# Hybrid encoder on one core: softmax normalised once per pair of heads, by rows that TensorE makes, instead of once per block of probabilities

## The chip, the cores and the metric

The kernel runs on one core of a Trainium2 chip. A core has TensorE (matrix products and transposes), VectorE, ScalarE, GpSimd and SyncE, which issues transfers; each runs its own queue of instructions in order. The metric is the device time in microseconds (us) of one execution. In the profile's rows PE is TensorE's matmul, PEld its weight load, DVE VectorE, ACT ScalarE, POOL GpSimd and SP SyncE; "SPq" is SyncE's DMA queue.

## The reference

Two layers over a sequence of 512 with width 1024; a conditioning vector gives shift, scale and gate for both halves of a layer. Attention has 8 dilated heads and 8 latent heads (MLA); then comes an MLP of width 4096. Shortened:

```python
for l in range(2):
    h = rms_norm(x, g_norm_mix) * (1 + sc1) + sh1
    q_d, k_d, v_d, cq, ckv, k_rope = split(h @ w_in)
    o_dil = dilated_attention(rms_norm(q_d), rms_norm(k_d), v_d, positions, slopes)  # 8 heads of 64
    o_mla = latent_attention(cq, ckv, k_rope, positions, ...)                        # 8 heads, rotary part of 32
    x = x + gt1 * (concat[o_dil, o_mla] @ w_out)
    h = rms_norm(x, g_norm_mlp) * (1 + sc2) + sh2
    x = x + gt2 * (relu(h @ w_mlp_in) ** 2 @ w_mlp_out)
# each head: p = exp(s - max s);  l = sum(p);  o = (p @ v) / l
```

A dilated head's score has a bias of slope times distance of the positions, and the mixture over three dilations comes down to one softmax with a further table of logarithms in the bias. The latent heads rotate 32 of their 96 score columns by angles of the positions.

## The kernel before, in words

**Layout.** Activations are transposed: x is 8 tiles of [128, 512], width on the partitions. For accuracy every operand of a product is split into a high and a low part: `load_split` loads a weight tile `raw` and makes `wh` (ScalarE, L233) and `wl` (GpSimd, L234). `mm3` issues three matmuls for each product (L238 to L240). All weights are streamed by SyncE.

**Attention.** Each layer has 8 stages `st`, one for each pair of heads: 0 to 3 dilated, 4 to 7 latent. `heads` runs `head` for both heads of the pair. A head has 4 steps, one for each block of 128 queries, 128 steps in the whole kernel. A step runs: score matmuls into `sc`; the maximum on VectorE (L346, or with the bias added in the same instruction, L343); the exponential on ScalarE, which also gives the sum l_ (L347, L344); the reciprocal r_ on VectorE (L348); P times r_, by a table `NRM` on ScalarE (L351, 56 steps), VectorE (L353, 8) or GpSimd (L355, 64); four transposes of P on TensorE (L358); a high copy on ScalarE (L361) and the low rest on VectorE (L362). Behind the four steps stand the products with the values (L368), and ScalarE and VectorE put the head's 64 rows into `o` (L370, L371). At the pair's end `o` is split into `ot`, high on ScalarE (L628) and low on GpSimd (L629). The output projection reads `ot`.

**What lies between the steps.** `weave` puts pieces of the next pair's projection, weight loads, the output projection's first half and layer 1's modulation between the steps, at places that the table `TUNE` gives. From this program a planner of the framework sets the final order on every engine, and the semaphores; a change of the code can therefore move instructions that it does not touch.

**Buffers.** Tiles of one tag share a ring of buffers (`BUFS`, L61): `s` has two, `P` three, `o` one. In PSUM, tag `mm` has four banks, `sc` (scores) two, `tr` (transposes of P, products with the values) two. A tile that takes a buffer waits for the last reader of the tile that had it.

**The start of layer 0's attention.** The latent part is transposed and split into `ct` tiles (`ot` tag, L527, L528). `rope_tables` makes the rotary tables of queries and keys from a gain `g` (loaded at L482) by five small GpSimd operations each (L487 to L491) into tiles `rot` of their own; L535 to L538 rotate the keys `kr` (written at L512). `distances` loads the row of positions `posr` into an `s` tile (L307); VectorE cuts it into 16-bit halves (L312, L313) and converts them (L314), and from these come the distances for the biases.

Of the kernel before, what the change touches and what calls it, by code (L numbers as in the profile page):

```python
# [9 lines left out]
F32 = mybir.dt.float32  # L10
F32R = mybir.dt.float32r
I32 = mybir.dt.int32
AF = mybir.ActivationFunctionType
# [15 lines left out]

NRM = (('AAGG', 'GAGA'), ('GAGA', 'GAVG'))

TUNE = dict(
    F0=(0, 0), F1=(6.4, 2.33), T0=(3.23, 2.08), T1=(8.8, 8.8), M0=(0, 0), M1=(4, 4), M2=(4.1, 4.1),
    M3=(6.5, 6.55), LD0=(5, 5), LD1=(9, 9), LM=(6.45, 7.11), LO=(7.2, 7.2), OD0=(3.1, 3.1), OD1=(5.1, 5.1),
# [6 lines left out]
def trunk(ctx: ExitStack, tc: tile.TileContext, a):  # L43
# [12 lines left out]
    def nm(p):  # L56
# [1 line left out]
        return f"{p}{uid[0]}"  # L58


    BUFS = dict(h=8, qk=8, ot=8, pt=4, zz=2, raw=3, wh=4, wl=4, P=3, b=2, s=2, o=1, st=9, hs=9,  # L61
                mm=4, sc=2, tr=2)

    def t4(tag, shape, dt=F32R):
# [259 lines left out]
        SY.dma_start(g, a["lnc"])  # L324
        return dist, g

    def head(l, h, hd, score, bias, vals, o):
        pt = [(t4("pt", [128, 4, 256]), t4("pt", [128, 4, 256])) for _ in range(2)]
        for qb in range(4):
            sc = ps("sc")  # L330
            score(hd, sc, qb)
            m, l_, r_ = (small(1, "hs") for _ in range(3))
            P = s2(tag="P")
            if bias:
                b = s2(tag="b")
                if l == 0:
                    dist, g = bias
                    A.activation(b, dist[qb // 2][:, qb % 2], AF.Abs, scale=SLOPES[h])
                    G.tensor_tensor(b, b, g[:, 384 - 128 * qb:896 - 128 * qb], op=OP.add)
                    SY.dma_start(bias_d[h][qb], b)  # L340
                else:
                    SY.dma_start(b, bias_d[h][qb])
                V.tensor_tensor_reduce(P, sc, b, op0=OP.add, op1=OP.min, scale=1.0, scalar=3e38, accum_out=m)  # L343
                A.activation(P, P, AF.Exp, bias=m, scale=-1.0, accum_out=l_)  # L344
            else:
                V.tensor_reduce(m, sc, axis=AX.X, op=OP.max, negate=True)  # L346
                A.activation(P, sc, AF.Exp, bias=m, scale=1.0, accum_out=l_)  # L347
            V.reciprocal(r_, l_)  # L348
            e_ = NRM[l][bool(bias)][qb]
            if e_ == "A":  # L350
                A.activation(P, P, AF.Copy, scale=r_)  # L351
            elif e_ == "V":
                V.tensor_scalar(P, P, r_, None, op0=OP.mult)  # L353
            else:
                G.tensor_scalar(P, P, r_, 0.0, op0=OP.mult, op1=OP.add)  # L355
            tr = ps("tr", (128, 4, 128))
            for kc in range(4):
                T.transpose(tr[:, kc], P[:, kc * 128:(kc + 1) * 128], ident)  # L358
            c0 = (qb % 2) * 128
            hi, lo = (t[:, :, c0:c0 + 128] for t in pt[qb // 2])  # L360
            A.activation(hi, tr, AF.Copy)  # L361
            V.tensor_tensor(lo, tr, f(hi), op=OP.subtract)  # L362
            yield
# [14 lines left out]
    for l in range(L):  # L378
# [99 lines left out]


        def rope_tables(src, is_k):  # L480
            g = col(NR, "gr")
            SY.dma_start(g, bass.AP(tensor=src.tensor, offset=src.offset, ap=[[0, 128], [1, NR]]))  # L482
            C = rot(2 * is_k)
            Sn = rot(2 * is_k + 1)
            ga = g[:, 0:16].rearrange("p (o d) -> p o d", o=1).to_broadcast([128, 4, 16])
            gb = g[:, 16:32].rearrange("p (o d) -> p o d", o=1).to_broadcast([128, 4, 16])
            G.tensor_tensor(C[:, :, 0], cos, ga, op=OP.mult)  # L487
# [134 lines left out]
        def heads(st, w):  # L622
            pr, bias = st % 4, (bias0 if l == 0 else True) if st < 4 else None
            o = s2(tag="o")
            for hd in range(2):
                yield from head(l, 2 * pr + hd, hd, w["score"], bias, w["vals"], o)
            ot = t4("h" if st in (2, 3) else "ot", [128, 2, S])
            A.activation(ot[:, 0], o, AF.Copy)  # L628
            G.tensor_tensor(ot[:, 1], o, f(ot[:, 0]), op=OP.subtract)  # L629
            OT.append(ot)  # L630
# [302 lines left out]
```

## Time and profile before

| | before |
|---|---|
| device time, median of 3 runs (all) | 1374.31 us (1374.08 to 1374.61) |
| profiled execution, its own time | 1371.87 us |
| span of its instructions | 1370.1 us |
| TensorE matmul busy | 1274.0 us, 93% |
| TensorE weight loads busy | 1106.1 us, 81% (beside the matmuls) |
| VectorE / ScalarE / GpSimd busy | 762.4 / 683.7 / 662.0 us (56 / 50 / 48%) |
| mean granted clock of TensorE | 0.974 |

Rows of the profile that group instructions give the line, engine, operation, what it writes and reads with shapes, the count, then busy time and the mean of one in ns, then the engine's idle time just before them and what ended it ("<-POOL P L355" is the write of P by GpSimd at line 355). Rows of single instructions begin with start and length in us, and end in brackets with the idle time before them. "x4" is a run of four. Rows of a stretch A:B give its length, then the busy time of PE, PEld, DVE, ACT and POOL, the granted clock (1.00 is full), the DMA engines' busy share and GB/s.

### The profile page before, as it was taken

How to read it: one execution, taken by the hardware profiler on the slowest of the kernel's cores; microseconds unless marked ns; L12 is line 12 of the kernel's file. 1: busy time of each engine (PE TensorE's matmuls, PEld its weight loads, DVE VectorE, ACT ScalarE, POOL GpSimd, SP SyncE). 2: the span in 40 equal slices, each digit the busy share in tenths (PEclk: the TensorE clock that was granted, in tenths of full speed). 3: DMA queues.
4: the chain of work that ended last, by engine and by line, in shares of the span. 5: the costliest groups of instructions: out<-in, count | busy, mean ns of one | idle time of the engine just before them, and what ended most of it. 6: DMA issues, size and time to landing. Idle time of an engine off the chain costs nothing.

```text
span 1370.1 us, 19443 instructions
## 1 busy us (share of the span) xinstructions
PE 1274.0 (93%) x6922; PEld 1106.1 (81%) x6922; DVE 762.4 (56%) x1732; ACT 683.7 (50%) x1453; POOL 662.0 (48%) x600
## 2 busy tenths in 40 slices
PE   3889878888999999999998999899889999999999
PEld 2877867777988888888888999788788888888888
DVE  6687887786653481743576577998562122121223
ACT  5578787876442231322235577888654233232321
POOL 5646686663454444444436244455246444444441
PEclk7989998999999999999999999999999999999999
DMA  9325553232235483754533244311013223222321
GB/s 344 112 88 184 165 160 101 87 108 73 98 123 185 149 280 108 235 203 133 181 124 89 89 122 145 93 47 47 17 62 106 94 93 101 99 92 97 104 92 62
DMA packets 57248, 167.61 MB, mean 122 GB/s; under 512 B 8640, under 2 KB 10816, under 8 KB 57152
## 3 DMA queue, kind: packets, MB, share of 16 engines
q1 hardware_dynamic: 57152, 166.38, 37.3%
q8 instruction: 54, 0.88, 0.3%
q14 instruction: 42, 0.34, 0.1%
HBM read 155.87 MB, written 10.49 MB: 121 GB/s over the span
## 4 chain that ended last, share of the span: by engine, by line
PE 73%; DVE 6%; ACT 6%; issue 4%; POOL 3%; DMA 3%; POOLq 0%; DVEq 0%; ACTq 0%
PE mm L238 21%; PE mm L239 21%; PE mm L240 21%; PE tr L368 2%; PE tr L358 2%; POOL wl L234 2%; DMA raw<-in_wout_dram 1%; DVE pt L362 1%; DVE raw L170 1%; DMA raw<-in_wup_dram 1%; ACT pt L361 1%; PE sc L238 1%; ACT P L347 1%; PE mm L603 1%; PE sc L239 1%
## 5 line engine op out<-in xcount | busy, mean ns | idle before, releaser
L234 POOL TENSOR_TENSOR wl<-raw,wh 128x1024 fp32r<-128x1024 f32 (+3 forms) x188 | 425.7, 2268 | 454.9 <-ACT wh L233 433.1
L233 ACT ACTIVATE wh<-raw 128x1024 fp32r<-128x1024 f32 (+3 forms) x188 | 188.7, 1004 | 272.6 <-PE mm L240 202.7
L636 DVE SCALAR_TENSOR_TENSOR x<-mm,mod,x 128x512 f32<-128x512 f32 (+1 forms) x144 | 89.3, 630 | 261.7 <-PE mm L240 261.2
L238 PE MATMUL mm<-h,wh 128*128 128x512 f32 (+1 forms) x608 | 224.5, 370 | 7.1 <-ACT h L274 7.1
L239 PE MATMUL mm<-h,wl 128*128 128x512 f32 (+1 forms) x608 | 224.4, 370 | 0.0
L240 PE MATMUL mm<-h,wh 128*128 128x512 f32 (+1 forms) x608 | 222.1, 369 | 1.6 <-POOL h L271 1.1
L238 PE MATMUL mm<-ot,wh 128*128 128x512 f32 (+1 forms) x448 | 155.2, 348 | 4.3 <-ACT ot L628 4.1
L239 PE MATMUL mm<-ot,wl 128*128 128x512 f32 (+1 forms) x448 | 154.0, 345 | 0.0
L240 PE MATMUL mm<-ot,wh 128*128 128x512 f32 (+1 forms) x448 | 152.6, 347 | 0.2 <-POOL ot L629 0.2
L809 ACT ACTIVATE P<-mm 128x512 f32<-128x512 f32 (+1 forms) x72 | 39.2, 551 | 203.2 <-PE mm L240 203.2
L238 PEld LDWEIGHTS mm<-h,wh 128*128 128x128 f32 x608 | 116.1, 191 | 25.9 <-ACT h L274 7.5
L240 PEld LDWEIGHTS mm<-h,wh 128*128 128x128 f32 x608 | 114.6, 190 | 21.1 <-POOL h L271 1.5
L239 PEld LDWEIGHTS mm<-h,wl 128*128 128x128 f32 x608 | 116.1, 191 | 19.1 <-POOL wl L234 0.3
L810 DVE SCALAR_TENSOR_TENSOR mm<-mm,P 128x512 f32<-128x512 f32 (+1 forms) x72 | 45.4, 635 | 139.5 <-ACT P L809 139.5
L238 PE MATMUL mm<-wh,h 128*128 128x384 f32 (+1 forms) x288 | 97.0, 352 | 16.5 <-ACT h L719 9.8
L238 PE MATMUL mm<-qk,wh 128*128 128x512 f32 (+1 forms) x288 | 105.2, 366 | 1.0 <-DVE x L636 1.0
L239 PE MATMUL mm<-qk,wl 128*128 128x512 f32 (+1 forms) x288 | 105.2, 365 | 0.0
L240 PE MATMUL mm<-qk,wh 128*128 128x512 f32 (+1 forms) x288 | 105.2, 365 | 0.0
L239 PE MATMUL mm<-wh,h 128*128 128x384 f32 (+1 forms) x288 | 99.8, 349 | 5.3 <-POOL h L722 3.2
L240 PE MATMUL mm<-wl,h 128*128 128x384 f32 (+1 forms) x288 | 99.3, 347 | 0.8 <-POOL wl L234 0.8
L170 DVE SCALAR_TENSOR_TENSOR pt<-pt,cb 128x1024 f32<-128x1024 f32 x56 | 99.2, 1806 | 0.0
L238 PEld LDWEIGHTS mm<-ot,wh 128*128 128x128 f32 x448 | 85.3, 190 | 15.2 <-ACT ot L628 4.5
(248 smaller groups left out, 2673.3 us busy)
## 6 DMA issues: line engine op xcount, KB each, us to landing
raw<-in_w_dram SPq DMA_DIRECT2D x64, 512.0 KB, 3.4
pt<-in_wmod_dram SPq DMA_DIRECT2D x56, 512.0 KB, 4.9
raw<-in_w2a_dram SPq DMA_DIRECT2D x48, 512.0 KB, 3.5
raw<-in_wmod_dram SPq DMA_DIRECT2D x24, 512.0 KB, 3.7
raw<-in_win_dram SPq DMA_DIRECT2D x30, 384.0 KB, 3.1
bias<-b SPq DMA_DIRECT2D x32, 256.0 KB, 2.3
raw<-in_wout_dram SPq DMA_DIRECT2D x16, 512.0 KB, 3.7
raw<-in_w2b_dram SPq DMA_DIRECT2D x16, 512.0 KB, 3.3
```

Of the source, the lines that this page charges most:

```text
L170: r = V.scalar_tensor_tensor(w, w, 1.0, cb, op0=OP.mult, op1=OP.mult, accum_out=out)
L233: A.activation(hi, raw, AF.Copy)
L234: G.tensor_tensor(lo, raw, f(hi), op=OP.subtract)
L238: T.matmul(out, sh, mh, start=first, stop=False)
L239: T.matmul(out, sl, mh, start=False, stop=False)
L240: T.matmul(out, sh, ml, start=False, stop=last)
L347: A.activation(P, sc, AF.Exp, bias=m, scale=1.0, accum_out=l_)
L358: T.transpose(tr[:, kc], P[:, kc * 128:(kc + 1) * 128], ident)
L368: T.matmul(po[:, HALF[qh]], vals(hd, kc), pt[qh][w][:, kc], start=(kc == 0 and w == 0), stop=(kc == 3 and w == 1))
L636: V.scalar_tensor_tensor(xT[j][:, hf], p, gt[:, j:j + 1], xT[j][:, hf], op0=OP.mult, op1=OP.add)
L809: A.activation(r, p, AF.Relu)
L810: V.scalar_tensor_tensor(p, p, 0.0, r, op0=OP.max, op1=OP.mult)
```

## The change

The scaling of P goes out. The sums of a pair's 8 steps go into one tile `den` [128, 8], queries on the partitions. At the pair's end VectorE inverts it into `rc`; ScalarE spreads the values into `wide` [128, 4, 2, 64] (an `s` tile); TensorE transposes the four blocks into a bank of tag `mm`, where the inverted sums now lie as rows along the queries, 64 equal rows for each head; VectorE multiplies `o` by them. Only then is `o` split. `o` gets a second buffer. Besides, the keys' rotary tables move from tiles of their own into an `s` tile, and the gain `g` of all four tables shares one buffer.

```diff
-NRM = (('AAGG', 'GAGA'), ('GAGA', 'GAVG'))
...
-    BUFS = dict(h=8, qk=8, ot=8, pt=4, zz=2, raw=3, wh=4, wl=4, P=3, b=2, s=2, o=1, st=9, hs=9,
+    BUFS = dict(h=8, qk=8, ot=8, pt=4, zz=2, raw=3, wh=4, wl=4, P=3, b=2, s=2, o=2, st=9, hs=6, den=4,
...
-    def head(l, h, hd, score, bias, vals, o):
+    def head(l, h, hd, score, bias, vals, o, den):
...
-            m, l_, r_ = (small(1, "hs") for _ in range(3))
+            m, l_ = small(1, "hs"), den[:, 4 * hd + qb:4 * hd + qb + 1]
...
-            V.reciprocal(r_, l_)
-            e_ = NRM[l][bool(bias)][qb]
-            if e_ == "A":
-                A.activation(P, P, AF.Copy, scale=r_)
-            elif e_ == "V":
-                V.tensor_scalar(P, P, r_, None, op0=OP.mult)
-            else:
-                G.tensor_scalar(P, P, r_, 0.0, op0=OP.mult, op1=OP.add)
...
         def rope_tables(src, is_k):
-            g = col(NR, "gr")
+            g = const.tile([128, NR], F32, tag="gr", name=nm("gr"))
             SY.dma_start(g, ...)
-            C = rot(2 * is_k)
-            Sn = rot(2 * is_k + 1)
+            if is_k:
+                both = s2([128, 2, 4, 2, 16])
+                C, Sn = both[:, 0], both[:, 1]
+            else:
+                C, Sn = rot(0), rot(1)
...
             o = s2(tag="o")
+            den, rc = small(8, "den"), small(8, "den")
             for hd in range(2):
-                yield from head(l, 2 * pr + hd, hd, w["score"], bias, w["vals"], o)
+                yield from head(l, 2 * pr + hd, hd, w["score"], bias, w["vals"], o, den)
+
+            V.reciprocal(rc, den)
+            wide = s2([128, 4, 2, 64])
+            A.activation(wide, rc.rearrange("p (h q o) -> p q h o", h=2, o=1).to_broadcast([128, 4, 2, 64]), AF.Copy)
+            rows = ps("mm", (128, 4, 128))
+            for qb in range(4):
+                T.transpose(rows[:, qb], wide[:, qb].rearrange("p h d -> p (h d)"), ident)
+            V.tensor_tensor(o, rows.rearrange("p q c -> p (q c)"), o, op=OP.mult)
             ot = t4("h" if st in (2, 3) else "ot", [128, 2, S])
```

In the changed kernel the lines before `head` stand two higher (L307 is L305, L312 is L310), those from the transposes of P on ten (L358 is L348, L362 is L352), and the split of `ct`, L528, is L521. New are L622 (reciprocal), L624 (spreading), L627 (transposes) and L628 (product).

The planner's order changes too. SyncE's queue at the start of layer 0's attention, before, with what each transfer waits for (`s_774` is the row of positions, `raw` are tiles of weights, `bias` a copy of a bias tile in memory):

```order
L165 DMA raw_886<-in_wmod_dram 128x1024 [waits DMAHW3_49,Pool_49]
L165 DMA raw_1015<-in_wmod_dram 128x1024 [waits DMAHW7_49,DMAHW4_49,Pool_49]
L232 DMA raw_1097<-in_win_dram 128x768 [waits DMAHW5_49,DMAHW0_49,Pool_49]
L307 DMA s_774<-in_pos_dram 128x512 [waits DVE_49,DMAHW1_49,PE_49,Activation_49]
L324 DMA ot_797<-in_lnc_dram 128x896 [waits DMAHW2_49]
L340 DMA bias_176<-b_812 128x512 [waits Pool_49]
```

The same place after (the row of positions is now `s_773`, `gr_7504` a gain for a rotary table):

```order
L163 DMA raw_879<-in_wmod_dram 128x1024 [waits DMAHW4_49,DMAHW0_49,Pool_49]
L163 DMA raw_1000<-in_wmod_dram 128x1024 [waits DMAHW2_49,Pool_49]
L230 DMA raw_1078<-in_win_dram 128x768 [waits DMAHW6_49,DMAHW3_49,Pool_49]
L472 DMA gr_7504<-in_gqr_dram 128x32 [waits DMAHW7_49,DMAHW1_49,Pool_49]
L305 DMA s_773<-in_pos_dram 128x512 [waits PE_49,DVE_49,Activation_49,Pool_49]
L322 DMA ot_796<-in_lnc_dram 128x896
L338 DMA bias_176<-b_811 128x512 [waits Pool_49]
```

The row of positions now waits for GpSimd (Pool) as well, and a gain's transfer, which waits too, has come in ahead of it. GpSimd's instruction in question is L530, the last one that reads the keys' tables (L537 before).

VectorE at the same place, before (`kr` keys, `pt` the halves of the positions, `ot` the split of `ct`):

```order
L512 TENSOR_SCALAR kr_635<-tr_209,st_689 128x32
L312 TENSOR_SCALAR pt_776<-s_774 128x512
L313 TENSOR_SCALAR pt_776<-s_774 128x512
L314 CAST pt_777<-pt_776 128x1024
L436 TENSOR_REDUCE st_893<-s_894 128x4
L528 SCALAR_TENSOR_TENSOR ot_731<-mm_726,cols_70,ot_731 128x512
L528 SCALAR_TENSOR_TENSOR ot_739<-mm_734,cols_70,ot_739 128x512
```

And after:

```order
L505 TENSOR_SCALAR kr_635<-tr_209,st_689 128x32
L310 TENSOR_SCALAR pt_775<-s_773 128x512
L311 TENSOR_SCALAR pt_775<-s_773 128x512
L426 TENSOR_REDUCE st_886<-s_887 128x4
L312 CAST pt_776<-pt_775 128x1024
L521 SCALAR_TENSOR_TENSOR ot_731<-mm_726,cols_70,ot_731 128x512
L521 SCALAR_TENSOR_TENSOR ot_739<-mm_734,cols_70,ot_739 128x512
```

The readers of the positions keep their place right behind `kr` and ahead of the splits of `ct`; one reduction of the first pair's projection has moved up by one.

GpSimd from there on, before (`wl` low parts of weights, `rot` and `s` the rotation of the keys and tables):

```order
L234 TENSOR_TENSOR wl_829<-raw_827,wh_828 128x768
L234 TENSOR_TENSOR wl_835<-raw_833,wh_834 128x768
L535 TENSOR_TENSOR rot_768<-kr_635,rot_761 128x128
L536 TENSOR_TENSOR s_769<-kr_635,rot_762 128x4x16
L537 TENSOR_TENSOR s_769<-kr_635,rot_762 128x4x16
```

And after:

```order
L232 TENSOR_TENSOR wl_832<-raw_830,wh_831 128x768
L480 TENSOR_TENSOR s_761<-cos,gr_759 128x4x16
L481 TENSOR_TENSOR s_761<-cos,gr_759 128x4x16
L482 TENSOR_TENSOR s_761<-sin,gr_759 128x4x16
L484 TENSOR_TENSOR s_761<-sin,gr_759 128x4x16
L483 TENSOR_SCALAR s_761<-s_761 128x4x16
L528 TENSOR_TENSOR rot_767<-kr_635,s_761 128x128
L529 TENSOR_TENSOR s_768<-kr_635,s_761 128x4x16
L530 TENSOR_TENSOR s_768<-kr_635,s_761 128x4x16
```

The five operations that make the keys' tables stood far earlier in GpSimd's queue and now stand right ahead of the rotation of the keys.

TensorE around the end of layer 0's first pair, before (`mm` is a projection of a later pair, `sc` the next pair's scores, `tr` transposes of P):

```order
L240 MATMUL mm_1360<-wl_1193,h_188 128x384
L468 MATMUL sc_1269<-qk_890,qk_889 128x512
L468 MATMUL sc_1307<-qk_890,qk_889 128x512
L358 MATMUL tr_1184<-ident,P_1175 128x128 x4
L238 MATMUL mm_1443<-wh_1098,h_184 128x384
```

And after:

```order
L348 MATMUL tr_1157<-ident,P_1150 128x128 x4
L348 MATMUL tr_1181<-ident,P_1174 128x128 x4
L458 MATMUL sc_1249<-qk_883,qk_882 128x512
L458 MATMUL sc_1283<-qk_883,qk_882 128x512
L627 MATMUL mm_1233<-ident,s_1231 128x128 x4
L236 MATMUL mm_1267<-wh_1079,h_184 128x384
```

The four transposes of the inverted sums stand behind the next pair's first scores and ahead of a projection of a later pair.

## The prediction

> **What bounds the kernel now.** I read the page first, then busy time by stretch, then TensorE's waits, then the instructions in order of time at the places that the change touches.
>
> ```profile
> span 1370.1 us, 19443 instructions
> PE 1274.0 (93%) x6922; PEld 1106.1 (81%) x6922; DVE 762.4 (56%) x1732; ACT 683.7 (50%) x1453; POOL 662.0 (48%) x600
> ```
>
> TensorE is busy for 93% of the span, so the change can only pay where it waits. The change acts on attention, which runs from about 75 to 342 us in layer 0 and from about 760 to 990 us in layer 1. The table of busy time by stretch (length, then busy us of each engine, granted clock, DMA share, GB/s) cuts it at pair ends.
>
> ```profile
> 105.00:137.00 32.00, 29.17 (x177) 25.20 (x176) 25.01 (x69) 25.80 (x61) 22.66 (x19) 1.00 0.61 190
> 137.00:168.00 31.00, 26.60 (x166) 24.76 (x166) 24.59 (x58) 23.21 (x55) 21.30 (x16) 1.00 0.51 166
> 168.00:201.00 33.00, 25.92 (x176) 22.66 (x175) 30.16 (x87) 29.48 (x74) 25.78 (x27) 0.98 0.55 174
> 201.00:228.00 27.00, 20.87 (x109) 16.76 (x110) 17.31 (x55) 21.95 (x57) 19.68 (x35) 0.78 0.36 118
> ...
> 310.00:342.00 32.00, 27.34 (x171) 22.64 (x169) 19.63 (x40) 19.45 (x40) 12.79 (x17) 1.00 0.23 72
> 105.00:342.00 237.00, 202.91 (x1234) 174.78 (x1232) 183.59 (x489) 183.30 (x441) 151.18 (x193) 0.95 0.39 125
> 775.00:852.00 77.00, 76.81 (x492) 74.41 (x492) 54.13 (x157) 53.98 (x131) 29.76 (x27) 1.00 0.41 121
> 852.00:899.00 47.00, 40.77 (x279) 34.15 (x278) 43.50 (x141) 39.78 (x109) 23.21 (x56) 1.00 0.34 103
> 899.00:966.00 67.00, 67.00 (x442) 59.84 (x441) 57.02 (x155) 55.22 (x138) 36.92 (x72) 1.00 0.14 43
> 966.00:990.00 24.00, 19.17 (x129) 15.99 (x129) 14.51 (x29) 16.96 (x36) 4.92 (x6) 1.00 0.04 16
> ```
>
> Two regimes. In layer 1, TensorE is full from 775 to 852 and from 899 to 966: nothing can be won there, and added matmuls cost their time. Idle is 6.2 us (852 to 899) and 4.8 us (966 to 990). In layer 0 no engine is full: TensorE lacks 2.8, 4.4, 7.1, 6.1 and 4.7 us in the first five rows and 34.1 in the row from 105 to 342, with VectorE and ScalarE near 80 to 90%. That is a chain that passes between engines, and layer 0 is where a shorter chain may pay.
>
> **Part 1: reciprocal and scaling leave the step.** Each of the 128 steps loses a reciprocal and a 128x512 multiplication. The groups by line (count, busy us, mean ns, then idle before and who ended it):
>
> ```profile
> L348 DVE RECIPROCAL hs<-hs 128x1 f32<-128x1 f32 x128 | 20.2, 158 | 20.0 <-ACT P L344 9.8 <-ACT P L347 9.0
> L351 ACT ACTIVATE P<-P,hs 128x512 f32<-128x512 f32 x56 | 40.4, 722 | 6.3 <-DVE hs L348 6.1
> L355 POOL TENSOR_SCALAR P<-P,hs 128x512 f32<-128x512 f32 x64 | 44.5, 695 | 81.9 <-DVE hs L348 75.2 <-PE sc L240 3.1 <-PE tr L358 2.1
> L353 DVE TENSOR_SCALAR P<-P,hs 128x512 f32<-128x512 f32 x8 | 4.1, 507 | 0.1
> L358 PE MATMUL tr<-ident,P 128*128 128x128 f32 x512 | 78.4, 280 | 17.5 <-DVE o L371 6.1 <-POOL P L355 4.8 <-DVE pt L362 3.5
> L358 PEld LDWEIGHTS tr<-ident,P 128*128 128x128 f32 x512 | 60.5, 143 | 31.6 <-POOL P L355 12.8 <-DVE o L371 9.4 <-ACT P L351 2.0
> ```
>
> Off the engines go 24.3 us of VectorE, 40.4 of ScalarE and 44.5 of GpSimd. What counts is the latency, seen in two steps of layer 0's last stage:
>
> ```profile
> 320.55 0.67 ACT L347 ACTIVATE P<-sc,hs 128x512 f32<-128x512 f32 x1
> 321.34 0.16 DVE L348 RECIPROCAL hs<-hs 128x1 f32<-128x1 f32 x1 [0.28 <-ACT P L347]
> 321.54 0.72 ACT L351 ACTIVATE P<-P,hs 128x512 f32<-128x512 f32 x1 [0.23 <-DVE hs L348]
> ...
> 327.13 0.69 ACT L347 ACTIVATE P<-sc,hs 128x512 f32<-128x512 f32 x1 [0.35 <-DVE hs L346]
> 328.27 0.69 POOL L355 TENSOR_SCALAR P<-P,hs 128x512 f32<-128x512 f32 x1 [0.99 <-DVE hs L348]
> ```
>
> From the exponential's end to the scaled tile it is 1.04 us (321.22 to 322.26) and 1.14 us (327.82 to 328.96). All 128 would be some 140 us; the trace shows how little of it is exposed. Directly, TensorE's matmul row blames scaling on GpSimd for 4.8 us; the weight-load row, whose idle begins earlier, blames the two scalings for 12.8 + 2.0 = 14.8. A wait of this sort averages about one removed step, so it goes nearly whole. Between 4.8 and 14.8 I take the middle, **10 us gained**: the matmul row misses what the load in front of it waited for, the load row counts time in which matmuls still ran.
>
> Indirectly, ScalarE and GpSimd have shorter queues, and weight splits and bias tiles behind a blocked scaling get through. Those 34.1 us and layer 1's 6.2 and 4.8 make about 45 that TensorE lacks; 10 of it are booked. Of the remaining 35 I give **6 us**: most is ended by VectorE, whose load falls little (24.3 us less, 13.5 more, below). The bounds are 0 and 15, half of what ScalarE is relieved by net (40.4 less some 10).
>
> **Part 2: what a pair's end adds.** Sixteen times: a reciprocal (0.16), a broadcast copy on ScalarE, four transposes, a VectorE product out of PSUM. The nearest rows of a copy, a PSUM product and four transposes followed by other matmuls:
>
> ```profile
> L811 ACT ACTIVATE ot<-P 128x512 fp32r<-128x512 f32 x28 | 17.4, 620 | 0.0
> L371 DVE TENSOR_TENSOR o<-tr,o 64x512 f32<-64x512 f32 x32 | 21.8, 682 | 9.5 <-ACT o L370 8.7
> ...
> 240.93 0.60 PE L358 MATMUL tr<-ident,P 128*128 128x128 f32 x4
> 241.28 1.19 PE L368 MATMUL tr<-pt,qk 128*128 128x256 f32 x8
> ```
>
> ScalarE gets 16 x 0.62 = 9.9 us, VectorE 16 x (0.16 + 0.68) = 13.5, both beside TensorE's work and inside the relief above. TensorE's four transposes occupy between 0.35 us (when the next matmul starts) and 0.60: 16 x 0.35 = **5.6 us lost**, at most 9.6; I take the lower since these follow other matmuls in the order. They are hidden only where TensorE idles anyway, so the low end is 2. At a layer's end the product is bare:
>
> ```profile
> 340.83 0.69 DVE L371 TENSOR_TENSOR o<-tr,o 64x512 f32<-64x512 f32 x1 [1.81 <-ACT o L370]
> 341.55 0.63 ACT L628 ACTIVATE ot<-o 128x512 fp32r<-128x512 f32 x1 [0.75 <-DVE o L371]
> 342.23 0.39 PE L238 MATMUL mm<-ot,wh 128*128 128x256 f32 x1 [2.06 <-ACT ot L628]
> ```
>
> TensorE sits idle for 2.06 us here; the product puts 0.68 and a hand-over of 0.08 into that gap, twice: **1.5 us lost**. The second o buffer I cost at nothing: no wait for its reader stands in L370's or L371's rows.
>
> **Part 3: the tables that moved.** The rotary tables of the keys now live in the two-buffer pool "s", and the row of positions, which takes the same slot, waits until GpSimd's L537 has read them. The start of layer 0's attention before:
>
> ```profile
> 82.57 0.33 SPq L307 DMA_DIRECT2D s<-in_pos_dram  x1
> ...
> 85.41 0.46 POOL L535 TENSOR_TENSOR rot<-kr,rot 128x128 f32<-128x128 f32 x1 [11.89 <-DVE kr L512]
> 86.10 0.32 POOL L537 TENSOR_TENSOR s<-kr,rot 128x64 f32<-128x64 f32 x1
> 86.33 0.43 DVE L312 TENSOR_SCALAR pt<-s 128x512 int32<-128x512 int32 x1 [1.00 <-DMA s<-in_pos_dram]
> 89.36 2.07 DVE L528 SCALAR_TENSOR_TENSOR ot<-mm,cols,ot 128x512 fp32r<-128x512 f32 x3 [0.16 <-ACT ot L527]
> 90.17 0.19 PEld L238 LDWEIGHTS mm<-wh,h 128*128 128x128 f32 x1 [2.05 <-DVE ot L528]
> ```
>
> The transfer left at 82.57; now it cannot leave before L537's end, 86.42, so 3.9 us later. VectorE runs in order, and its first reader stands in the same place in its queue, ahead of the L528 splits that free the bank for TensorE. TensorE's pause of about 2 us there becomes 5.7 to 5.9, all of it on the path. Nothing in its order stands between. A pause of that length also cost clock elsewhere:
>
> ```profile
> 379.92 0.39 PE L238 MATMUL mm<-h,wh 128*128 128x256 f32 x1 [3.53 <-ACT h L274]
> ...
> 379.90:383.50 3.60, 3.58 (x18) 3.58 (x19) 3.22 (x9) 2.74 (x6) 2.88 (x5) 0.57 0.02 5
> 199.50:209.50 10.00, 6.76 (x23) 4.98 (x24) 3.91 (x15) 6.42 (x16) 8.87 (x14) 0.50 0.48 166
> ```
>
> After 3.53 us of idling the granted clock was 0.57 for 3.6 us: at best 1.6 us of TensorE lost. I take half, 0.8, as VectorE is nearly the limit at that place: **4.7 us lost**, between 2 (if later VectorE work catches up) and 5.5. The Trainium skill (TensorE: Matmul & The Clock Gate, section "What's actually happening") says that an idle window of about 3.4 us puts the array's clock at half until a like stretch of work; the pair of rows at 379.9 agrees, and the rule speaks against this edit: by it the whole 1.6 us is due, and the sum below would be 0.8 us worse.
>
> The same move takes the keys' tables, a few small GpSimd operations, from in front of a weight split that TensorE waited for at the start:
>
> ```profile
> 59.98 0.65 PE L240 MATMUL sc<-wl,h 128*128 128x416 f32 x2 [1.02 <-POOL wl L234]
> ```
>
> They go where GpSimd idles for 11.89 us (the row of L535 above). **1 us gained**, 0 to 1.
>
> **Sum.** -10 - 6 - 1 + 5.6 + 1.5 + 4.7 = -5.2 us. The profiled execution took 1371.87 us (1.8 around its span), hence 1366.7. It is 2.4 us under the runs' median of 1374.31, so I forecast **1369 us** for the median.
>
> **Rivals.**
> *A dense TensorE (1361 us).* The row at 199.5 to 209.5 shows a clock of 0.50 for 10 us, in which TensorE was still busy for 6.8. If the shorter chain fills those holes, half of the 6.8 comes back, and relief reaches its bound of 15 instead of 6: -5.2 - 3.4 - 9 = -17.6 at the most; I price it half way, -13. For it: scalings wait for 75 us on GpSimd. Against: L343 and L361 remain in series. By the clock rule of the Trainium skill's page named above (same section), every hole closed below one window also saves a half-rate spell, which is this case.
>
> *It changes nothing (1375 us).* The next thing in line (L371's release of the transposes' bank, L362) is late by as much: only the matmul row's 4.8 goes, relief is 4: -4.8 - 4 - 1 + 11.8 = +2.0 at the profiled execution, within a run's noise of the median when the delay at 90 us is partly caught up: +0.7.
>
> *Slower (1379 us).* The way of the sums crosses three in-order queues (VectorE, ScalarE, TensorE) 16 times, and its transposes stand in TensorE's queue ahead of the next stage's work. If the broadcast copy is late there, TensorE stalls with everything behind it. At 0.65 us each it is 10.4 us: -5.2 + 10.4 = +5.2. It decides from 0.33 us per pair. For it: the copy stands behind other ScalarE work, busy for 80 to 90%. Against: the transposes' bank is not needed at once.
>
> **How the numbers follow.** Forecast's case 0.42 (1366 to 1371.5), dense 0.16, nothing 0.22, slower 0.20. To the range belong the forecast and most of the rivals: 1362 to 1380, which leaves out half of the dense case and a tail of the slow one. Faster by over 0.2% (below 1371.6; 2.7 us is about what a measurement tells) is 0.42 + 0.16, less a little: 0.57; within it 0.23; slower 0.20.
>
> **What would show it.** L348's, L351's and L355's rows are gone; the transposes' weight loads have GpSimd nowhere in their idle; the transfer of the positions leaves near 86.5 us and TensorE pauses for 5 to 6 us before 94, with a clock below 1.0 behind it; the stretch from there to the end of layer 0's attention is at least 10 us shorter; the pause before the output projection grows from 2.06 to about 2.8 us. I am wrong if the transposes' idle goes over to L362 or L371 at the same size, or if TensorE's waits name the broadcast copy.

## The result and the profile after

The changed kernel takes 1407.11 us (median of 4 runs, 1403.73 to 1415.12) against 1374.46 us before (median of 4): ratio 1.0242, 95% interval 1.0205 to 1.0280. Forecast was 1369 us, 1362 to 1380. The profile after is of the slowest of the four runs, 1415.12 us, so its span is some 8 us longer than that of a middle run.

The head of the page after:

```profile
span 1413.3 us, 19324 instructions
PE 1301.0 (92%) x6986; PEld 1131.0 (80%) x6986; DVE 763.9 (54%) x1628; ACT 664.4 (47%) x1413; POOL 614.0 (43%) x536
```

GpSimd's busy time fell by 48 us, ScalarE's by 19, and VectorE's rose by 1.5. Booked were falls of 44.5, of 30 (40.4 less 9.9) and of 11 (24.3 less 13.5). The rows of the instructions that went and came bear these sums out on ScalarE (40.4 less 10.0) and VectorE (24.3 less 14.0). An engine's busy time counts a moment in which two of its instructions overlap only once, so it can fall by less than the work. The kernel's time went up all the same.

The time lost has two parts. TensorE's idle time, span less busy, grew from 96.1 to 112.3 us: 16 of the 43 us by which the span grew. Its busy time grew by 27.0 us, of which the new transposes have at most the 11.6 of their row (below). Most of the rest is the same matmuls taking longer at a lower mean clock, 0.959 against 0.974; busy time times the missing share of the clock, summed over slices of 5 us, gives an estimate of 23 us before and 42 after.

Cut at the ends of attention (length, busy us of PE, PEld, DVE, ACT, POOL, granted clock, DMA share, GB/s), first before, then after:

```profile
75.00:342.00 267.00, 228.93 (x1370) 198.07 (x1368) 208.53 (x561) 205.37 (x515) 162.02 (x207) 0.94 0.38 119
760.00:989.00 229.00, 217.40 (x1407) 196.97 (x1405) 178.02 (x512) 176.09 (x447) 101.78 (x163) 1.00 0.27 82
989.00:1370.00 381.00, 373.13 (x1888) 319.44 (x1888) 101.41 (x182) 115.86 (x173) 164.54 (x81) 1.00 0.28 90
```

```profile
75.00:354.00 279.00, 238.18 (x1393) 210.91 (x1394) 209.54 (x511) 191.67 (x487) 136.07 (x175) 0.90 0.36 115
772.00:1027.00 255.00, 232.19 (x1460) 205.31 (x1459) 177.10 (x457) 171.08 (x441) 81.26 (x137) 0.99 0.23 74
1027.00:1413.00 386.00, 377.13 (x1895) 323.64 (x1894) 101.38 (x182) 116.03 (x172) 164.32 (x81) 0.98 0.27 89
```

Attention of layer 0 became 12 us longer, that of layer 1, where TensorE had been nearly full, 26 us, and the rest behind it 5 us. The groups of the steps and of the pair ends after:

```profile
L348 PE MATMUL tr<-ident,P 128*128 128x128 f32 x512 | 82.3, 286 | 35.0 <-ACT P L342 12.2 <-DVE o L361 9.1 <-ACT P L345 6.4
L627 PE MATMUL mm<-ident,s 128*128 128x128 f32 x64 | 11.6, 313 | 1.1 <-ACT s L624 1.1
L628 DVE TENSOR_TENSOR o<-mm,o 128x512 f32<-128x512 f32 x16 | 10.9, 684 | 0.2
L624 ACT ACTIVATE s<-den 128x512 f32<-128x512 f32 x16 | 10.0, 624 | 0.3 <-DVE st L224 0.3
L622 DVE RECIPROCAL den<-den 128x8 f32<-128x8 f32 x16 | 3.1, 195 | 1.4 <-ACT P L342 1.3
```

The new instructions take about the time that was booked for them, and TensorE waits 1.1 us for the spread sums in all. But the idle time before the transposes of P doubled, from 17.5 to 35.0 us. Over half of it, 18.6 us, is now ended by the exponentials (L342, L345), which write P last now; of the scaling, which did so before, the row of before names GpSimd's with 4.8 us. TensorE stands at the transposes, and the next thing in its queue is not ready. Where its filler went can be seen at one place. The 15 us ahead of the second pair's last product with the values in layer 1, instructions that write `mm` tiles alone (projections and their transposes; after, also the four of L627), before and after:

```profile
835.00:850.00 15.00, 10.89 (x62) 9.83 (x60) 3.57 (x11) 3.06 (x9) 1.00 0.45 126
```

```profile
844.50:859.50 15.00, 4.91 (x29) 4.36 (x29) 2.88 (x7) 1.62 (x4) 1.00 0.48 154
```

TensorE's instructions in order of time at that place after:

```profile
846.30 0.50 PE L458 MATMUL sc<-qk,qk 128*128 128x512 f32 x1 [0.79 <-DVE hs L341]
...
847.60 1.10 PE L358 MATMUL tr<-pt,qk 128*128 128x256 f32 x7 [0.44 <-DVE pt L352]
...
850.52 0.66 PE L348 MATMUL tr<-ident,P 128*128 128x128 f32 x4 [0.73 <-DVE o L361]
...
852.83 0.73 PE L459 MATMUL sc<-qk,qk 128*128 128x512 f32 x2 [0.42 <-DVE qk L450]
853.50 0.66 PE L348 MATMUL tr<-ident,P 128*128 128x128 f32 x4
853.99 0.60 PE L627 MATMUL mm<-ident,s 128*128 128x128 f32 x4
854.35 0.42 PE L236 MATMUL mm<-wh,h 128*128 128x384 f32 x1
```

Before, 62 such matmuls fill the waits of the pair's last steps, and TensorE is busy for all of the 15 us (12.6 after). After, TensorE waits four times in 7 us, then makes the pair end's rows (L627), and only behind them does the next projection begin. The same can be counted in the built programs: matmuls that stand in TensorE's queue ahead of a pair's last product with the values, though the program writes them behind it. Summed over the 16 pairs there are 890 before and 281 after (60 of these are the pair ends' own transposes). I call this number the run-ahead.

### The profile page after: what moved, and what is told of

Read it like the earlier page. It is cut to its first block, busy times and chain, and to the rows that moved or that the text cites. A ratio compares the mean times of both kernels' runs of the same rounds, so it can differ in the third digit from the quotient of the medians.

```text
span 1413.3 us, 19324 instructions
## 1 busy us (share of the span) xinstructions
PE 1301.0 (92%) x6986; PEld 1131.0 (80%) x6986; DVE 763.9 (54%) x1628; ACT 664.4 (47%) x1413; POOL 614.0 (43%) x536
## 4 chain that ended last, share of the span: by engine, by line
PE 76%; DVE 8%; ACT 7%; DMA 3%; issue 3%; POOL 3%; DVEq 0%; POOLq 0%; ACTq 0%
PE mm L237 22%; PE mm L236 22%; PE mm L238 21%; PE tr L358 4%; PE tr L348 2%; DMA raw<-in_wout_dram 1%; ACT wh L231 1%; POOL wl L232 1%; DVE pt L352 1%; PE sc L236 1%; DMA b<-bias 1%; ACT pt L351 1%; PE sc L237 1%; PE sc L238 1%; ACT P L345 1%
## 5 line engine op out<-in xcount | busy, mean ns | idle before, releaser
L236 PE MATMUL mm<-h,wh 128*128 128x512 f32 (+1 forms) x608 | 227.2, 375 | 6.7 <-ACT h L272 6.7
L238 PE MATMUL mm<-h,wh 128*128 128x512 f32 (+1 forms) x608 | 224.8, 373 | 0.0
L236 PE MATMUL mm<-ot,wh 128*128 128x512 f32 (+1 forms) x448 | 157.9, 353 | 4.9 <-DVE o L628 4.4
L238 PE MATMUL mm<-ot,wh 128*128 128x512 f32 (+1 forms) x448 | 153.7, 348 | 0.0
L236 PEld LDWEIGHTS mm<-h,wh 128*128 128x128 f32 x608 | 119.0, 196 | 25.7 <-ACT h L272 7.1
L238 PEld LDWEIGHTS mm<-h,wh 128*128 128x128 f32 x608 | 117.5, 194 | 19.3 <-POOL h L269 0.3
L236 PE MATMUL mm<-wh,h 128*128 128x384 f32 (+1 forms) x288 | 99.4, 358 | 17.0 <-ACT h L721 9.8
L348 PE MATMUL tr<-ident,P 128*128 128x128 f32 x512 | 82.3, 286 | 35.0 <-ACT P L342 12.2
L237 PE MATMUL mm<-wh,h 128*128 128x384 f32 (+1 forms) x288 | 102.6, 357 | 5.3 <-POOL h L724 3.1
L348 PEld LDWEIGHTS tr<-ident,P 128*128 128x128 f32 x512 | 61.5, 146 | 53.9 <-ACT P L342 16.6
L352 DVE TENSOR_TENSOR pt<-tr,pt 128x512 fp32r<-128x512 f32 x128 | 87.1, 684 | 29.3 <-ACT pt L351 28.8
```

What stands on the lines that cost most here:

```text
L236: T.matmul(out, sh, mh, start=first, stop=False)
L237: T.matmul(out, sl, mh, start=False, stop=False)
L238: T.matmul(out, sh, ml, start=False, stop=last)
```

## The experiments

Theories: **order** (the new order of TensorE is the loss), against **pair end** or **work** (the added instructions and their waits are the loss). When the first had won, a second pair of theories asked what makes the order: **bank** (a pair end claims one of the four `mm` banks) or its place in the **program**. Each ratio is to the kernel before on the same chip, with its 95% interval.

**Without scaling**: before, less the lines of r_ and the scaling.

```diff
-            V.reciprocal(r_, l_)
-            e_ = NRM[l][bool(bias)][qb]
... (and the three branches)
```

> The kernel before without the reciprocal and without the scaling of P; nothing takes their place, so the softmax is left unnormalised. The planner is free to order everything anew. Theory 'order' (the planner's new order on TensorE is what costs the time, since pieces of the next pair are no longer put between an exponential and its transposes): no gain from shorter steps, 1375 to 1400 us. Theory 'pair end' (the sums' way through VectorE, ScalarE and TensorE at the end of a pair, with a bank of the projections held meanwhile, is what costs): this kernel has no pair end and is faster than before, 1355 to 1366 us.

1371.83 us, 0.9976 (0.9964 to 0.9988). Both theories missed: the whole removal is worth 3.3 us, far from the 16 that the prediction booked, but it is no loss. The idle time before P's transposes, 17.5 us before, did not fall:

```profile
L350 PE MATMUL tr<-ident,P 128*128 128x128 f32 x512 | 77.2, 278 | 20.3 <-DVE o L363 7.0 <-ACT P L344 5.6 <-DVE pt L354 5.1
```

**The same, TensorE in the order of before.** Held orders are made with edges between successive instructions of the engine, which ask for no wait:

```diff
+ tc.add_manual_dep(mine[b], mine[a].name, DependencyInfo(NoSync, DATA))   # a, b: neighbours in the old order
```

> The same as the kernel without scaling, but TensorE's instructions are held in the order that they have in the kernel before; the other engines are ordered by the planner around that. Softmax unnormalised. Theory 'order': the gain that the prediction booked for the shorter step comes out here, 10 to 16 us, 1358 to 1365 us, and clearly less than the kernel without scaling and with a free order. Theory 'pair end': equal to the free one within 5 us.

1377.74 us, 1.0018 (1.0004 to 1.0032). Both theories missed here too: there is no gain of 10 to 16 us, and the two kernels without scaling lie 5.9 us apart, a little over the 5 allowed. In before's order, steps shorter by a microsecond gain nothing: its order had hidden the scaling. The run is also the nearest control for the holding itself, since no kernel was held in its own order: a held order with less work stands 0.2% above before.

**Without the pair end**: the changed kernel, less L622 to L628.

> The changed kernel without the reciprocal, the spreading, the transposes and the product at a pair's end; softmax unnormalised. The tables' move, the two output buffers and the tile of sums stay. Theory 'order': still slow, 1390 to 1405 us. Theory 'pair end': about 1360 to 1370 us, so that the pair end accounts for 35 to 45 us. If it stands half way, both share.

1363.74 us, 0.9919 (0.9901 to 0.9937). 'Pair end' holds so far: it alone turns 1363.7 into 1407.1, by 43 us. Without it the idle time before P's transposes is below that of before:

```profile
L348 PE MATMUL tr<-ident,P 128*128 128x128 f32 x512 | 78.8, 280 | 12.0 <-DVE o L361 5.0 <-DVE pt L352 3.8 <-ACT P L342 1.6
```

**Before's work in the order of after**: before, TensorE held in the changed kernel's order.

> The kernel before, scaling and all, but with TensorE's instructions held in the order that the planner gave them in the changed kernel (the pair end's transposes do not exist here). Theory 'order': the time goes up although no work was changed, to 1395 us or more. Theory 'pair end': within 8 us of before, 1374 to 1382 us.

1434.13 us, 1.0435 (1.0408 to 1.0462). No instruction added or taken away, and 59 us lost by the order alone.

**No pair end, but in the order of after**: the kernel of 1363.7 us with TensorE held in the changed kernel's order.

> The changed kernel without the pair end (softmax unnormalised), as in the run of 1363.7 us, but TensorE held in the order that the planner gave it in the changed kernel, with only the 64 transposes of the pair ends left out. Theory 'order' (the pair end costs by making the planner order TensorE differently): 1390 to 1405 us, nearly the changed kernel's 1407. Theory 'waits' (the order is harmless and the added work and its waits cost): 1363 to 1372 us.

1407.05 us, 1.0233 (1.0213 to 1.0252), against 1.0242 (1.0205 to 1.0280) for the changed kernel: the same time within the spread (that the medians agree to a tenth is luck). The row of P's transposes shows its picture too:

```profile
L348 PE MATMUL tr<-ident,P 128*128 128x128 f32 x512 | 81.6, 285 | 33.3 <-ACT P L342 9.0 <-DVE pt L352 8.6 <-DVE o L361 8.4
```

So in this order the pair end's instructions cost nothing measurable on top. Both theories hold, one through the other: the pair end is the cause, and it acts by the order that the planner makes around it. The 6922 matmuls here are those of the kernel without a pair end in its free order; of the 44 us between the two profiled spans, 27 are more idle time of TensorE (114.1 against 86.9 us) and 17 more busy time, at a mean clock of 0.968 against 0.975.

**A light pair end.**

```diff
-            wide = s2([128, 4, 2, 64])
+            wide = s2([128, 2, 64])
...
-            rows = ps("mm", (128, 4, 128))
-            for qb in range(4): T.transpose(rows[:, qb], ...)
-            V.tensor_tensor(o, rows..., o, op=OP.mult)
+            rows = ps("mm", (128, 128))
+            T.transpose(rows, wide..., ident)
+            V.tensor_tensor(o[:, 0:1], rows[:, 0:1], o[:, 0:1], op=OP.mult)
```

> The changed kernel with a pair end of a quarter of the work: one spreading of 128x128, one transpose, and a product of one column instead of 512 (the softmax is not normalised). The order of dependences stays, and so does the time for which a bank of the projections' ring is held, from the transpose until the pair's output exists. Theory 'bank' (one of the four banks is held for some 7 us at each pair's end, so the planner and the chip can't run the next pair's projections ahead): 1393 to 1407 us, although most of the added work is gone. Theory 'work' (TensorE's transposes and VectorE's product cost): a quarter to a third of the 43 us stays, 1373 to 1380 us.

1405.60 us, 1.0224 (1.0184 to 1.0264); run-ahead 252. A quarter of the work costs the same.

**The bank freed early.**

```diff
+            rw = s2(tag="rw")
+            A.activation(rw, rows..., AF.Copy)
-            V.tensor_tensor(o, rows..., o, op=OP.mult)
+            V.tensor_tensor(o, rw, o, op=OP.mult)
```

> The changed kernel with the rows copied from the bank into an own tile by ScalarE at once, and the product taken from there; one output buffer pays for the tile. All the work stays and a copy of 0.6 us comes on top for each pair, but the bank is held for about 1.5 us instead of about 7. Theory 'bank': 1366 to 1380 us. Theory 'work': as slow as the changed kernel or slower, 1405 to 1415 us.

1404.82 us, 1.0214 (1.0190 to 1.0238); run-ahead 340. By its numbers this spoke for 'work' (1405 to 1415 us), which the light pair end rules out. So the holding time behind the transposes isn't what matters. That leaves the claim itself, and the next run moves it.

**The rows in the ring of P's transposes**: `ps("mm", ...)` becomes `ps("tr", ...)`.

> The changed kernel with the rows in the ring of the transposes of P (two banks) instead of the projections' ring (four banks). Nothing else is changed, and the planner is free. Theory 'bank': the projections get their bank back, but one of only two banks for the steps is now held, so the loss moves: 1380 to 1410 us. Theory 'work': equal to the changed kernel within 5 us, 1402 to 1412 us.

1385.89 us, 1.0090 (1.0057 to 1.0122); run-ahead 695. One word in the code gives back 21 of the 43 us.

**The spread sums out of the ring 's' as well**: `wide = s2([128, 4, 2, 64], tag="P")`, the rows in `tr` or in `sc`.

> The changed kernel with the rows in the two-bank ring of P's transposes (tr) and the spread sums in the three-buffer ring of P instead of the rings 'mm' and 's', which the projections of later pairs use. Work and chain are the same. Theory 'ring order' (slots of a ring are given out in program order, so a later pair's projection can't be placed ahead of a pair end that asked for a slot of the same ring earlier in the program and still waits for its sums): 1363.7 us without a pair end, plus 5.6 for the 64 transposes and 1.5 at the layers' ends, so 1371 us, 1366 to 1376. Theory 'work' (what remains is the pair end's own work and waits): as the run with the rows alone moved, 1382 to 1391 us.

> The same with the rows in the two-bank ring of the scores (sc). Theory 'ring order': 1366 to 1378 us; the scores' ring is taken by the next pair's first scores, which may wait a little longer. Theory 'work': 1382 to 1391 us.

1383.68 us, 1.0066 (1.0047 to 1.0085), and 1396.54 us, 1.0156 (1.0136 to 1.0175). The run-ahead is 866 and 884, that of before, and yet 20 and 33 us are missing against no pair end: a miss of 'ring order', whose ranges ended at 1376 and 1378 us; the first lies in the range of 'work', the second above it. A high run-ahead doesn't suffice. In the first run, half of the 20 us is idle time of TensorE (97.1 against 86.9 us), and the new transposes have 9.6 us of busy time. I take the idling for steps that wait for a bank of a two-bank ring, since TensorE idles 15.5 us before P's transposes against 12.0; no run shows that by itself.

**The tables alone**: before with the changed `rope_tables`.

> The kernel before with nothing changed but the tables: the keys' rotary tables in an 's' tile, one buffer for the gains. The prediction booked 4.7 us lost and 1 us gained: 1377 to 1379 us. Rival (the late row of positions is made up later, or the planner's order around it is as good): 1372 to 1376 us. The run without a pair end has the tables moved and is faster than the kernel that only leaves out the scaling (1363.7 against 1371.8 us), which speaks for the rival.

1375.87 us, 1.0002 (0.9988 to 1.0016). No measurable loss.

**All the work in before's order**: rows in `tr`, TensorE held in the order of before.

> The changed kernel with all its work, the rows in the ring of P's transposes, and TensorE held in the order of the kernel before (the 64 transposes are put in where the planner likes). Without the pair end's work and with the tables not moved, this order gave 1377.7 us. Theory 'order': the added work costs little once the order is good: 1377 to 1387 us. Theory 'work': the transposes and waits cost as much as in the changed kernel, 1395 us or more.

1423.12 us, 1.0353 (1.0330 to 1.0376): a miss of theory 'order' taken by itself (1377 to 1387 us); it lies where 'work' put it. The row says where the time goes:

```profile
L348 PE MATMUL tr<-ident,P 128*128 128x128 f32 x512 | 79.6, 282 | 28.7 <-DVE o L361 21.0 <-DVE pt L352 5.5 <-DVE st L223 1.4
```

P's next transposes wait 21 us for L361 to release a bank (6.1 for the same release before). My reading is that an order fits one set of claims on banks, and that `tr` has a claim here that this order doesn't know.

**Three banks and no pair end**: `mm=4` becomes `mm=3` in the kernel of 1363.7 us.

> The changed kernel without the pair end (softmax unnormalised) and with three banks instead of four in the projections' ring; the fourth stays empty. In its order only 298 of TensorE's matmuls that belong to later pieces of the program stand ahead of a pair's last product with the values, as against 717 with four banks (1363.7 us) and 281 in the changed kernel (1407 us). Theory 'bank' (a pair end that claims a bank of this ring leaves the projections with three, and that is the loss): 1395 to 1410 us with no pair end at all. Theory 'program order' (three banks would do, what hurts is that the claim stands ahead of the later projections): 1364 to 1380 us.

1420.45 us, 1.0322 (1.0287 to 1.0357); run-ahead 298. Without any pair end, one bank less costs 57 us, more than the whole change and more than 'bank' had named (1395 to 1410 us); 'program order', 1364 to 1380 us, is far off. So a bank too few in this ring is enough for such an order and such a loss. That a pair end, which claims its bank only for a time, loses its 43 us in this way is not shown by this run: for it speak the runs with the rows in other rings, and the next run shows that the place of the claim counts too.

**The pair end written later**: the block runs among the next pair's steps, three steps on, with `wide` in tag `o`.

```diff
-            V.reciprocal(rc, den) ... OT.append(ot)
+            def finish(): V.reciprocal(rc, den) ... OT.append(ot)
+            ends.append(finish)
...
-            ev = []
+            ev = [(3.05, ends.pop())] if ends else []
```

> The changed kernel with the pair end written three steps later in the program, among the next pair's steps, and the spread sums in the ring of the output buffers; the rows stay in the projections' ring. 593 matmuls of later pieces stand ahead of the pairs' last products instead of 281. Theory 'order': between the run with 281 (1407 us) and the one with 717 plus the transposes' 7 us (1371 us), by their line some 1381 us, so 1374 to 1390. Theory 'bank': the bank is still one of four and is held, 1395 to 1410 us.

1393.97 us, 1.0140 (1.0123 to 1.0158); run-ahead 593. Between the two expectations: the place in the program matters for a part of it, since some 13 us come back with the same claim made later. (With the spread sums in `o` alone, the block at its old place, the run-ahead is 316; its time was not measured.)

**Tables and two output buffers**: before with both.

> The kernel before with the tables moved and with two output buffers, scaling of each step kept. The prediction costed the second output buffer at nothing: as the tables alone, 1373 to 1378 us. Rival: the second buffer lets the next pair's output begin before the pair's split is done, and is part of why the kernel without a pair end (1363.7 us) is faster than the one that only leaves out the scaling (1371.8 us): 1364 to 1371 us.

1377.44 us, 1.0012 (0.9997 to 1.0027). The second buffer is worth nothing measurable.

**Rows by transfers.**

```diff
-            wide = ...; rows = ps("mm", ...); T.transpose(...) x4
+            for hd in range(2):
+                SY.dma_start(drow[hd]..., rc[:, 4 * hd:4 * hd + 4])
+                SY.dma_start(rows[64 * hd:64 * hd + 64], drow[hd]...to_broadcast([64, S]))
```

> The changed kernel with the pair end's rows made without TensorE, ScalarE and PSUM: the inverted sums go to memory by a transfer for each head, and come back spread over 64 partitions by another, issued by SyncE; one output buffer pays for the tile of rows. 751 matmuls of later pieces stand ahead of the pairs' last products. Theory 'bank': without a claim on a bank most of the 43 us go, 1364 to 1376 us, dearer at the layers' ends by the two transfers' latency (some 5 us each by the bias transfers' 2.3 us, an estimate). Rival: SyncE's queue waits for the sums and holds the weights' loads behind them, 1380 to 1400 us.

1497.04 us, 1.0873 (1.0837 to 1.0909), a bad miss. The transfers' rows (KB each, median us from issue to landing):

```profile
rw<-drow SPq DMA_DIRECT2D x32, 128.0 KB, 5.3
drow<-den SPq DMA_DIRECT2D x32, 2.0 KB, 10.6
```

Both theories missed. The way there and back takes 15.9 us where the expectation had allowed some 5. A run-ahead of 751 and no claim on a bank did not help. Whether that latency or SyncE's queue behind it makes up the 133 us was not separated.

**The rows in the output's own bank**: the second head's bank of products takes the transposes once VectorE has read it, so nothing more is claimed; `wide` in tag `o`, or in tag `P`.

```diff
-                T.transpose(rows[:, qb], ...)
+                T.transpose(w["po"][:, qb * 128:(qb + 1) * 128], ...)
```

> The changed kernel with the rows written into the bank that held the second head's product with the values, after VectorE has read it, so that the pair end claims no bank of its own; the spread sums lie in the ring of the output buffers. All the work stays. 793 matmuls of later pieces stand ahead of the pairs' last products. The price is in the chain: at each pair's end the transposes now come after the output instead of before it. Theory 'bank': the best of the complete kernels, 1363.7 plus 5.6 for the transposes plus 2 x 1.5 at the layers' ends, 1372 us, 1367 to 1380. Rival (the bank of P's transposes, held some 2 us longer at 16 places, costs as in the run with the rows in that ring): 1380 to 1388 us.

> The same with the spread sums in the ring of P instead of the output buffers' ring; 746 matmuls of later pieces stand ahead. It tells how far two orders of the same work lie apart. Theory 'bank': 1367 to 1382 us, within 6 us of the other. Rival: 1380 to 1388 us, as the other.

1381.70 us, 1.0046 (1.0032 to 1.0060), and 1385.96 us, 1.0080 (1.0050 to 1.0110); run-ahead 793 and 746. Both lie in the rival's range (1380 to 1388 us) and the first is above that of 'bank' (1367 to 1380), the second above its 1382. The first has the lowest median of the kernels that normalise at a pair's end, 25 us better than the changed one and still 6 behind before; its interval overlaps with that of the 1383.68 us run. Its own cost is seen in part:

```profile
L627 PE MATMUL tr<-ident,o 128*128 128x128 f32 x64 | 9.9, 277 | 4.8 <-DVE o L362 4.7
```

From their start to that of the next matmul, or to the end of their record where TensorE idles behind them, four transposes occupy 0.35 to 0.74 us in this trace, some 8 for all, and TensorE idles 4.8 us before them: some 13 of the 18 us by which it stands above the kernel without a pair end. The rest stays open.

## Why the prediction was wrong, point by point

**The step that failed is Part 2's sum for a pair's end.** It booked 5.6 us for the transposes and 1.5 at the layers' ends, 7.1 in all; the pair end measures 43 (1407.11 against 1363.74 us). What the sum added up, the time of the new instructions on each engine, was nearly right: 10.0 us on ScalarE against 9.9, VectorE 0.684 and 0.195 us each against 0.68 and 0.16, and on TensorE 0.35 to 0.76 us a pair from the transposes' start to the next matmul's, 7.6 us for all, against 5.6. It had no term for what they claim: a bank of the projections' ring, asked for in the program ahead of the next projections and given back at the pair's very end. The missing term is some 36 us. The run of 1407.05 us shows that it can act through the planner's order alone: that order costs the 43 us with no pair end in it. How much of it is the claim on this ring is bounded by the runs with the rows in banks of `tr`: 21 to 25 us come back there, and 18 to 22 stay with the pair end even so. The rival "slower" had the sign, by another mechanism: it feared the broadcast copy, for which TensorE waited 1.1 us in all. Its counter-argument, that the bank is not needed at once, is the sentence that was most wrong.

The other parts together come to -12.3 us (-10 - 6 - 1 + 4.7), and the kernel with all of the change but the pair end measures -11.4 (1363.74 against 1375.17 us). That points at Part 2 as well, but the close fit is in part luck, since the single steps don't bear out their terms.

**Part 1 alone doesn't measure what was booked.** 10 us direct and 6 indirect were booked; the removal measures 3.3 us with a free order and none in the old one. Waits ended by scaling (4.8 and 14.8 us in the two rows) were taken as nearly whole gains. What came next in line was late as well: in the row of the kernel without scaling, L363, the exponential L344 and L354 end 17.7 us of idle time, and in before's order the time is even 0.2% longer. The rival "it changes nothing", which left 8.8 of the 16 us, was nearer on this part. Two readings of the prediction were off besides: VectorE and ScalarE are busy for 61 to 91% of the rows shown and 77% of the row from 105 to 342, not 80 to 90%, and half way between -5.2 and -17.6 is -11.4, not the -13 of the dense rival.

**Part 3 had the mechanism right and the loss in the wrong place.** The transfer leaves late, and TensorE pauses. Behind the pause that stood here before, the clock was full:

```profile
90.00:100.00 10.00, 9.83 (x59) 9.66 (x60) 8.73 (x25) 8.09 (x21) 4.63 (x4) 1.00 0.14 52
```

After the change:

```profile
85.39 0.33 SPq L305 DMA_DIRECT2D s<-in_pos_dram  x1
...
89.04 0.43 DVE L310 TENSOR_SCALAR pt<-s 128x512 int32<-128x512 int32 x1 [4.79 <-DMA s<-in_pos_dram]
...
91.45 0.69 PE L236 MATMUL mm<-wh,h 128*128 128x384 f32 x1 [3.49 <-DVE ot L521]
...
91.50:98.50 7.00, 7.00 (x25) 7.00 (x26) 6.48 (x12) 3.15 (x6) 3.41 (x2) 0.57 0.11 44
```

VectorE waits 4.79 us instead of 1.00, as worked out. TensorE's pause, by the matmul's row, grew from 1.81 to 3.49 us (the prediction's 2.05 is the weight load's), not to 5.7. The transfer left 2.8 us later, not 3.9, since the last of the keys came 1.1 us earlier (84.01 against 85.09). VectorE made up about half of that: its splits began at 90.65 instead of 89.36. The clock behind the pause was 0.57 for 7 us. With the tables alone the same pause stands there, 3.17 us, with a clock of 0.76 for 7 us behind it:

```profile
92.46 0.69 PE L238 MATMUL mm<-wh,h 128*128 128x384 f32 x1 [3.17 <-DVE ot L531]
```

Yet the tables alone cost 0.85 us between medians, within the interval. 4.7 us were booked. The delay is made up elsewhere, or offset by the new order; no run tells which.

**At the layers' ends** the added product is there, as forecast, and TensorE's pause grew less than the 0.76 us expected, from 2.06 to 2.22 us in layer 0:

```profile
351.96 0.68 DVE L361 TENSOR_TENSOR o<-tr,o 64x512 f32<-64x512 f32 x1 [2.54 <-ACT o L360]
352.68 0.69 DVE L628 TENSOR_TENSOR o<-mm,o 128x512 f32<-128x512 f32 x1
353.40 0.63 ACT L630 ACTIVATE ot<-o 128x512 fp32r<-128x512 f32 x1 [1.48 <-DVE o L628]
353.52 0.55 PE L236 MATMUL mm<-ot,wh 128*128 128x256 f32 x1 [2.22 <-DVE o L628]
```

The second output buffer, costed at nothing, was worth nothing measurable. Of the other signs that were named: GpSimd is gone from the idle time of the transposes, as said; attention in layer 0 is 12 us longer instead of 10 shorter; and the idle time went mostly to the exponentials (18.6 us), while L371's share (L361 now) grew from 6.1 to 9.1 us and the broadcast copy has 1.1, so that the two ways named in which it could go wrong describe little of it.

**The banks.** The three rings of this kernel hold 4 + 2 + 2 banks, and with three in the first it loses 57 us. The Trainium skill (PSUM — Partial Sum Buffer, "PSUM: the matmul accumulator") says that a core has eight banks of this size and that TensorE can write nowhere else. By that a transpose always claims a bank, and here all eight were given out; the page doesn't price a bank, the run of 1420 us does.

**Left open.** The kernel without a pair end is 8 us faster than the one without scaling, though tables and second buffer, the main differences, measure nothing when the scaling is kept. I take it for the spread between the planner's orders (the last two runs, the same work in two orders, lie 4.3 us apart, with intervals that overlap), but no run isolates it. What of the 18 us between the rows in the output's own bank and no pair end at all is work, and what order, is open too.

## What to carry to other kernels

Price a new step by the buffers that it claims, not only by its engine time: who else takes slots of that ring, what is written behind the claim in the program, and how long the claim waits for its inputs. Where a planner sets the order, count in the built program how much later work still stands ahead of the long chains: this count fell from 890 to 281 here, and could be read before any run. It warns and doesn't rank: every kernel with a count of 340 or less took over 1404 us, but the fastest, without a pair end, had 717, and two with 866 and 884 were slower. A short latency removed from a chain that is already filled with other work gained nothing here in the old order, and 3.3 us in a new one.

## What the runs showed of the hardware

Runs of one kernel can differ with the granted clock: the changed kernel's four runs had spans of 1413.3, 1406.3, 1404.3 and 1401.9 us at mean clocks of 0.959, 0.961, 0.966 and 0.967, the longer, the lower the clock, and 11 us apart. It is not so in each kernel: without a pair end, the fastest of four runs (1361.89 us) has the lowest clock, 0.975 against 0.981 and 0.982. The Trainium skill (TensorE: Matmul & The Clock Gate, "What's actually happening") says that the window in which activity is watched runs freely, so where a pause falls in it differs from run to run; differences between runs of one kernel fit with that, but no run here shows the window itself. And a transfer of 2 KB in pieces of 4 bytes (32 of them took the packets under 512 bytes from 8640 to 26048) took 10.6 us to land, three times as long as 512 KB of weights (3.4 us on the page of before).
